# A two-layer hybrid trunk on one core: two low parts of pointwise weights on VectorE, and four pieces of work queued later

## The chip, the core and the metric

The kernel is one program on one core of a Trainium2 chip. The metric is the device time of one execution in microseconds (us). A core has five engines, each of which works through a queue of its own in order: TensorE (PE in the profile; PEld are its weight loads) for matmuls, VectorE (DVE), ScalarE (ACT), GpSimd (POOL), and SyncE (SP), which here only issues transfers. An instruction starts when it is at the head of its queue and the semaphores that it waits for have come.

## The reference

512 positions of 1024 channels pass through two layers. Layer 0 mixes the positions with a gated delta rule (8 heads of 128), layer 1 with a Conformer convolution; each layer then attends to a fixed memory of 256 rows and applies an MLP with a squared ReLU. Every part begins with an RMS norm and ends with a residual sum. All is float32. What the change touches lies around the convolution:

```python
h = h + gated_deltanet(rms_norm(h, dn_norm), ...)                # ends with  o @ w_out
h = h + memory_cross_attention(rms_norm(h, xa_norm[0]), rms_norm(mem, xa_mem_norm[0]), ...)
h = h + sq_relu_mlp(rms_norm(h, mlp_norm[0]), ...)               # square(relu(h @ w_up)) @ w_down
...
u = rms_norm(h, cv_norm) @ w_pw1 + b_pw1                         # 1024 -> 2048
u = u[..., :1024] * sigmoid(u[..., 1024:])
c = causal_depthwise_conv(u, w_dw) + b_dw                        # 31 taps for each channel
c = silu(layer_norm(c, ln_g, ln_b))
h = h + c @ w_pw2 + b_pw2
h = h + memory_cross_attention(rms_norm(h, xa_norm[1]), rms_norm(mem, xa_mem_norm[1]), ...)
```

## The kernel before

**Weights in two parts.** A float32 product is made of three matmuls on a rounded form (fp32r): each operand is split into a high part and a low part, and high x high, low x high and high x low are summed (lines 316 to 318 for activations x weights). The weights come in units of 128 x 1024 (half a block of 1024 x 256). For each unit SyncE loads `raw` (six buffers), ScalarE makes the high part `wh` (a copy with a cast, line 257), and then VectorE or GpSimd makes the low part `wl` = `raw` - `wh` (line 73 is the helper of all elementwise operations on two tensors). There are three buffers of `wh` and `wl` (`NW`), so a cast waits until TensorE has finished with the unit three back. `wnext` hands the next unit of the plan `order` to TensorE and first splits the units up to `ready` ahead; `wsplit` makes one split. `POOL_LO` lists the units whose low part GpSimd makes, counted from `conv0`, the first unit of the convolution's first pointwise product.

**Who sets the order.** Each engine's queue is made by a scheduler that follows the order in which the program issues instructions, within limits: an instruction issued under `tc.issue_after(x)` is not queued ahead of x. `behind_merge` and the entries `ws["rb"]`, `ws["silu"]` and `ws["tap"]` are such gates for casts and low parts. The lists `CONV_SEQ` and `CONV_AFTER` set by hand what is issued after which unit of the convolution's stage.

**The end of the MLP in layer 0.** `mlp7` makes the down projection in four groups of seven products each (`product`); TensorE's matmuls there are `dn`. Their sums `acc` are merged, then `outs` turns them back into the channel layout (`hT`, line 306), adds the residual (`h`), and hands each tile of 128 channels to the norm of the next part: `parts` makes the high part `xh` (ScalarE, line 434) and the low part `xl` (VectorE, line 79), `square` makes the squares and adds them up. `outs(range(4))` runs inside the last product, `outs(range(4, 8))` (called `rest`) inside the first unit of the convolution's pointwise product, between its fourth and fifth k tile. `stat` then makes the norm's factor: matmuls `ssq` (line 453), a root `sd` on ScalarE (line 455), a reciprocal `rb` on VectorE. `mem_gain(1, 0)` and `mem_gain(1, 1)` scale the memory's two halves for the attention of layer 1 (high part `mh` on ScalarE, low part `ml` on VectorE).

**The convolution.** `pw_mm` makes the 16 units of the first pointwise product (`pw`); `pw_ev` evicts one tile of 128 channels: `sg` and `pa` are the two halves times `rb`, `sg` goes through the sigmoid (line 1482). Four tiles are convolved by taps: each tap is one operation on VectorE (`ca`, line 1537) or, for one tile, a ScalarE product and a GpSimd sum (`cvp`, `ca`). The other four go through TensorE: `pw_ev` clears a margin of two columns per phase in `gl` (memset, line 1495), writes the gated tile behind it, ScalarE's queue issues the transfer to DRAM (`gd`, line 1501), SyncE the one back, and `conv` makes the sums by matmuls (`cyp` on VectorE adds the bias). `gl` comes from a pool of three buffers; in this stage `cyp` holds two, so consecutive `gl` use one buffer. While the taps run, TensorE makes K and V of layer 1's attention (`kv_unit`, 16 more units). `moments` makes the layer norm's sums per position; two sums over partitions are matmuls `ln` that TensorE makes inside `kv_unit` at places 27 and 29 of `CONV_SEQ`. Then `ln_out` normalises, and the second pointwise product (`pw2`) begins.

Of the kernel before, what the change touches and what calls it, by code (L numbers as in the profile page):

```python
# [8 lines left out]
F32 = mybir.dt.float32  # L9
F32R = mybir.dt.float32r  # L10
AF = mybir.ActivationFunctionType
# [5 lines left out]
NTAP = 4  # L17
# [21 lines left out]
def tile_trunk(ctx, tc, xT, memT, x_d, mem_d, prm_d, adt_d, bdw_d, tap_d, fin_d, first_d, w_ab, w_kq, w_v, w_z, w_dno, w_pw1, w_pw2,  # L39
# [206 lines left out]
    def wsplit():  # L246
        u = ws["split"]
        ws["split"] += 1
        while ws["load"] <= need[u]:
            wload()  # L250
        (kind, i, *j), hf = order[u]
        raw = combos7(i, j[0], hf) if kind == "dn7" else ws["raw"].pop(need[u])
        h = wp.tile([P, 1024], F32R, tag="wh", name=nm("wh"), bufs=NW)
        lo = wp.tile([P, 1024], F32R, tag="wl", name=nm("wl"), bufs=NW)
        silu = kind == "pw2" and "silu" in ws
        with tc.issue_after(ws["silu" if silu else "rb"].ins) if silu or u in (3, 4) else behind_merge():
            ins = [act.copy(h, raw)]  # L257
        if u < 3:
            tc.keep_in_program_order(ins[0])
        gp = u - conv0 in POOL_LO  # L260
        with tc.issue_after(ws["tap"].ins) if "tap" in ws else nullcontext():
            ins.append(tt(pool if gp else dve, lo, raw, h.bitcast(F32), ALU.subtract))
        if not gp:
            ws["ins"] = ins[1]
        if u < 3:
            tc.keep_in_program_order(ins[1])
        ws["hl"][u] = (h, lo)
        if kind == "dn7":
            after7(i, j[0], hf)

    def wnext(key, hf):
        i = ws["next"]
        assert order[i] == (key, hf), (order[i], key, hf)
        while ws["load"] <= need[min(i + NRAW + 1 + 2 * (order[i][0][0] in ("up", "dn7")), len(order) - 1)]:
            wload()
        ready = NW - (order[i] == (("do", 1), 1)) if i > 2 else (1, 2, 1)[i]
        while ws["split"] < min(i + ready, len(order)):
            wsplit()
        ws["next"] += 1
        return ws["hl"].pop(i)  # L280
# [3 lines left out]
    def behind_merge():  # L284
        return tc.issue_after(ahead[0].ins) if ahead else nullcontext()

    T7 = {}

    def combos7(layer, g, u):
        name, h = order7(layer, g)[u // 2][1], u % 2  # L290
# [68 lines left out]
    def proj_moving(w, hf, q, xs, pss, cs_=None, inside=None):  # L359
        for c, ps in enumerate(pss):  # L360
            if cs_ is not None and c not in cs_:
                continue
            cs = slice(c * P, (c + 1) * P)
            for kk in range(2):
                k = q * 4 + hf * 2 + kk
                xh, xl = xs[k]
                s = slice(kk * 512, (kk + 1) * 512)
                pe.matmul(ps, xh[:, cs], w[0][:, s], start=k == 0, stop=False)
                pe.matmul(ps, xh[:, cs], w[1][:, s], start=False, stop=False)
                pe.matmul(ps, xl[:, cs], w[0][:, s], start=False, stop=k == KT - 1)  # L370
                if inside and c == kk == 0:
                    inside()

    def split(src, s):
        h = slot(F32R, s + "h")
# [48 lines left out]
    class Norm:  # L424
# [6 lines left out]

        def parts(self, t, h, pin=lambda i: i):
            xh = slot(F32R, "xh")
            pin(act.activation(xh, h, AF.Copy, scale=pc(self.g, t)))
            xl = slot(F32R, "xl")
            pin(stt(xl, h, pc(self.g, t), xh.bitcast(F32), ALU.mult, ALU.subtract))
            self.xs.append((xh, xl))

        def square(self, h, e=pool):
            sq = slot(s="sq")  # L440
# [38 lines left out]
    class DeltaNet:  # L479
# [474 lines left out]
        def heads_out(self, hs):  # L954
            pss = [[psum("ogT") for _ in range(2)] for _ in range(2)]
            for k, h in enumerate(hs):
                for c in range(4):
                    turn_in(pss[k // 2], (4 * (k % 2) + c) * 64, self.OG[h // 4, c][:, (h % 4) * P:(h % 4 + 1) * P])
            for k, h in enumerate(hs):
                oh, ol = slot(F32R, "oh"), slot(F32R, "ol")  # L960
                for o, lo, x in zip(by_half(oh), by_half(ol), turned_of(pss[k // 2], k % 2)):
                    act.activation(o, x, AF.Copy, scale=pc("out_norm"))
                    stt(lo, x, pc("out_norm"), o.bitcast(F32), ALU.mult, ALU.subtract)
                os_.append((oh, ol))

        def head_out(self, h):
# [237 lines left out]
    def mlp7(layer, norm, hres, nxt=None, mid=None):  # L1204
# [45 lines left out]
        def dn7(g, ops):  # L1250
# [10 lines left out]
            def product(i):  # L1261
                if (layer, g, i) == (0, 3, 6):
                    outs(range(4))
                left, right, key, opens = order7(layer, g)[i]
                if opens:
                    bank[key] = [psum("dn") for _ in range(2)]
                ws_ = [wnext(("dn7", layer, g), 2 * i)]
                if layer == 1 and (g, i) == (3, 6):
                    ws_.append(wnext(("dn7", layer, g), 13))
                    for h in range(2):  # L1270
                        part(left, ws_[h], bank[key][0], 0, h, opens)
                    held = []
                    evict(right, 0, bank[key][0], held)
                    return last_tile(left, ws_, held[0])
                todo = [(0, 0), (1, 0), (0, 1), (1, 1)]
                for c, h in todo:
                    if h == len(ws_):
                        ws_.append(wnext(("dn7", layer, g), 2 * i + 1))
                    part(left, ws_[h], bank[key][c], c, h, opens)
                    if h == 1:  # L1280
                        evict(right, c, bank[key][c])
# [51 lines left out]
        def outs(tiles):  # L1333
            todo = [(n, c, i) for n in range(2) for c in range(2) for i in tiles]
            pss = [[psum("hT") for _ in range(2)] for _ in range(2)]
            for n, c, i in todo:
                turn_in(pss[i // 2 % 2], (4 * (i % 2) + 2 * n + c) * 64, acc[n, 1 - i // 4, c][:, i % 4 * P:i % 4 * P + P])
            for k, i in enumerate(tiles):
                hn = slot(s="h")
                for o, x, r in zip(by_half(hn), turned_of(pss[i // 2 % 2], i % 2), by_half(hres[i])):  # L1340
                    tt(dve, o, x, r, ALU.add)
                new[i] = hn
                if k:
                    nxt.parts(i - 1, new[i - 1])
            nxt.parts(i, hn)
            for k in range(3) if i == 3 else range(3, 8):
                nxt.square(new[k], pool if i == 3 else dve)

# [107 lines left out]
    def conformer(norm, hres, nxt, rest):  # L1456
# [22 lines left out]
        def pw_ev(m):  # L1479
            sg = slot(s="sg")  # L1480
            tt(dve, sg, st.pop((m, 1)), norm.rb, ALU.mult)
            act.activation(sg, sg, AF.Sigmoid, bias=pc("b_pw1", 8 + m))
            a = slot(s="pa")
            tt(dve, a, st.pop((m, 0)), norm.rb, ALU.mult)
            if m < NTAP:
                x = wp.tile([P, 544], F32, tag="cv", name=nm("xn"), bufs=NCV)[:, 0:542]
                pool.memset(x[:, 0:30], 0.0)
                stt(a, a, pc("b_pw1", m), sg, ALU.add, ALU.mult)
                act.copy(phased(x[:, 30:542]), by_phase(a))
                (todo if m else todo_p).extend((dve_conv if m else pool_conv)(m, x))  # L1490
                return
            gl, x = [t.rearrange("p (j t) -> p j t", t=34) for t in (
                fsp.tile([P, 1024], F32, tag="fs", name=nm("gl"))[:, 0:544],
                wp.tile([P, 544], F32, tag="cv", name=nm("xg"), bufs=NCV))]
            dve.memset(gl[:, :, 0:2], 0.0)
            stt(gl[:, :, 2:34], by_phase(a), pc("b_pw1", m), by_phase(sg), ALU.add, ALU.mult)
            x16[m] = x, gl, drp.tile([P, PH, 34], F32, tag="gd", name=nm("gd"))

# [164 lines left out]
        def ln_out(m):  # L1663
            if m < NTAP:
# [3 lines left out]
                a = slot(s="la")  # L1668
                silu = act.activation(a, ps, AF.Silu, scale=pc("ln_g", m), bias=pc("ln_b", m))
                if m == NTAP - 1:  # L1670
                    ws["silu"] = silu
                return halves_of(a, m % 2 == 0)
            las.extend(slot(s="la") for _ in range(4))
            pss = [[psum("lnT") for _ in range(2)] for _ in range(2)]
# [14 lines left out]
        for i, (kind, u) in enumerate(CONV_SEQ):  # L1689
            if kind == "p":  # L1690
                pw_mm(*divmod(u, 2))
                if u % 2 and u > 1:
                    pw_ev(MORD[u // 2])
            else:
                kv_unit(1, u, lnw.pop("sum", None) if i in LN_SUM else None)

            for ins in gate:
                stack.enter_context(tc.issue_after(ins.ins))
# [216 lines left out]
    for m in range(8):  # L1915
# [1 line left out]
    n2 = Norm("mlp_norm0")  # L1917
    h = xattn(0, n1, h, n2)
    n3 = Norm("cv_norm")
    h, rest = mlp7(0, n2, h, n3, lambda: (mem_gain(1, 0), mem_gain(1, 1), taps(NTAP, *range(9)), selections()))  # L1920
    n4 = Norm("xa_norm1")
    h = conformer(n3, h, n4, rest)
    n5 = Norm("mlp_norm1")
# [49 lines left out]
TAPS_U = (4,) * 7 + (6,) * 9 + (3,) * 8 + (0,) * 8  # L1973
TAPS_C = {4: 0, 5: 0, 6: 0, 7: 0}
SHARE = 5
POOL_LO = (1, 2, 7, 8, 10, 11, 12, 13, 14, 15, 16, 18, 20)
MORD = (0, 1, 4, 2, 5, 3, 6, 7)
CONV_SEQ = [("p", i) for i in range(16)] + [("k", i) for i in range(16)]
CONV_AFTER = [(6, ("w", 4)), (7, ("r", 4)), (10, ("w", 5)), (12, ("r", 5)), (14, ("w", 6)), (15, ("r", 6)), (17, ("w", 7)), (18, ("r", 7)),
# [3 lines left out]
LN_SUM = (27, 29)  # L1983
CONV_AFTER += [(_i, ("t", _m, *range(_a, _a + 3))) for _i, _m, _a in (
    (2, 4, 9), (3, 5, 0), (4, 5, 3), (9, 5, 6), (10, 5, 9), (10, 6, 0), (11, 6, 3), (13, 6, 6), (14, 6, 9), (14, 7, 0), (15, 7, 3),
    (16, 7, 6), (17, 7, 9))]
# [103 lines left out]
```

## Time and profile before

| | |
|---|---|
| median of three runs | 1444.1 us |
| the three runs | 1446.07, 1441.85, 1444.1 us |
| the profiled execution | 1445.35 us |
| its span in the profile | 1443.6 us |
| mean granted clock of TensorE | 0.998 |
| busy share of the span: PE, DVE, ACT, POOL | 99%, 73%, 53%, 17% |

The span runs from the first to the last instruction of the profile; the 1.75 us between it and the profiled execution's time lie around it. Times within the profile are counted from the span's start: the output projection of layer 0's mixer begins at about 327, the first pointwise product at 789, the taps on VectorE at 823, the end of the convolution's stage lies at about 933. A row of a timeline gives the start, the duration, the engine, the line and operation, what is written and read, shapes, and a count where rows are grouped; brackets give the idle time of the engine just before, and what released it. The name `xl` of a helper's line can stand for tiles of several norms, so time and shape tell which is meant.

### The profile page before, as it was taken

What the parts mean: (1) busy time and instruction counts of PE and PEld (TensorE: products, weight loads), DVE (VectorE), ACT (ScalarE), POOL (GpSimd) and SP (SyncE); (2) the same over time, 40 slices, a digit from 0 to 9 for tenths busy, and PEclk for the clock granted to TensorE, in tenths of its full rate; (3) what the DMA queues carried; (4) which work ended last, traced back from release to release, by engine and by line L of the source; (5) the groups of instructions that cost most, each with busy time, mean ns of one, the idle gap of its engine ahead of it and who ended that gap; (6) DMA issues with size and microseconds to landing.
All of it is one profiled execution on the core that took longest, in us unless ns stands there. A gap on an engine that the chain in (4) does not pass through costs nothing.

```text
span 1443.6 us, 20463 instructions
## 1 busy us (share of the span) xinstructions
PE 1429.9 (99%) x7786; PEld 1194.4 (83%) x7786; DVE 1058.0 (73%) x1627; ACT 760.6 (53%) x1279; POOL 246.9 (17%) x246
## 2 busy tenths in 40 slices
PE   9999999999999999999999999999999999999998
PEld 7887888888888888888887887888888888888886
DVE  5989999878555766767679798985555766767677
ACT  6657856655444454444355655574444544444354
POOL 1212200102113010010002377211113010010101
PEclk9999999999999999999999999999999999999999
DMA  8232234522214576575766457743215476585853
GB/s 296 76 117 72 69 96 161 190 86 90 73 47 128 147 180 170 146 204 138 195 165 211 141 162 240 228 146 102 72 46 142 121 179 171 139 211 139 220 151 88
DMA packets 71860, 207.83 MB, mean 144 GB/s; under 512 B 15441, under 2 KB 16593, under 8 KB 71761
## 3 DMA queue, kind: packets, MB, share of 16 engines
q1 hardware_dynamic: 60960, 169.22, 36.0%
q0 software_dynamic: 9792, 35.66, 14.4%
q10 hardware_dynamic: 1008, 1.64, 0.3%
q8 instruction: 61, 1.00, 0.3%
q14 instruction: 39, 0.31, 0.1%
HBM read 203.28 MB, written 3.21 MB: 143 GB/s over the span
## 4 chain that ended last, share of the span: by engine, by line
PE 91%; DVE 6%; ACT 1%; issue 1%; DMA 0%; DVEq 0%; ACTq 0%
PE up L316 8%; PE up L318 8%; PE up L317 8%; PE dn L1259 7%; PE dn L1257 7%; PE dn L1258 7%; DVE ca L1537 3%; PE h L316 3%; PE h L317 3%; PE h L318 3%; PE xo L317 2%; PE q L317 2%; PE q L316 2%; PE xo L316 2%; PE xo L318 2%; PE q L318 2%
## 5 line engine op out<-in xcount | busy, mean ns | idle before, releaser
L257 ACT CAST wh<-raw 128x1024 fp32r<-128x1024 f32 x259 | 271.5, 1051 | 324.4 <-issue 93.8
L73 DVE TENSOR_TENSOR wl<-raw,wh 128x1024 fp32r<-128x1024 f32 (+1 forms) x249 | 307.0, 1235 | 90.0 <-ACT wh L257 88.6
L316 PE MATMUL up<-xh,wh 128*128 128x512 f32 x512 | 199.3, 389 | 0.0
L318 PE MATMUL up<-xh,wl 128*128 128x512 f32 x512 | 199.2, 389 | 0.0
L317 PE MATMUL up<-xl,wh 128*128 128x512 f32 x512 | 199.2, 389 | 0.0
L316 PEld LDWEIGHTS up<-xh,wh 128*128 128x128 f32 x512 | 96.1, 188 | 20.1
L317 PEld LDWEIGHTS up<-xl,wh 128*128 128x128 f32 x512 | 96.1, 188 | 20.0
L318 PEld LDWEIGHTS up<-xh,wl 128*128 128x128 f32 x512 | 96.1, 188 | 19.9
L244 POOL DMA_DIRECT2D t<-w_dn x48 | 42.1, 916 | 376.2 <-DVE wl L73 257.2
L1257 PE MATMUL dn<-wh,ah 128*128 128x512 f32 (+1 forms) x260 | 100.6, 387 | 0.0
L1259 PE MATMUL dn<-wl,ah 128*128 128x512 f32 (+1 forms) x260 | 100.4, 386 | 0.0
L1258 PE MATMUL dn<-wh,al 128*128 128x512 f32 (+1 forms) x260 | 100.4, 386 | 0.0
L79 DVE SCALAR_TENSOR_TENSOR rl<-up,rb 128x512 f32<-128x512 f32 x64 | 44.1, 690 | 58.6 <-PE up L318 58.6
L257 ACT CAST wh<-t 128x1024 fp32r<-128x1024 f32 x44 | 46.4, 1056 | 56.7 <-PE dn L1258 42.0
L73 DVE TENSOR_TENSOR wl<-t,wh 128x1024 fp32r<-128x1024 f32 x44 | 53.7, 1224 | 30.3 <-ACT wh L257 30.1
L1537 DVE SCALAR_TENSOR_TENSOR ca<-xn,prm,ca 128x512 f32<-128x512 f32 x85 | 64.0, 753 | 8.0 <-issue 3.4
L73 POOL TENSOR_TENSOR sq<-sq,sq 128x512 f32<-128x512 f32 x26 | 41.5, 1597 | 156.9 <-ACT sq L441 142.2
L73 DVE TENSOR_TENSOR acc<-acc,dn 128x512 f32<-128x512 f32 x99 | 66.6, 682 | 0.9
L316 PE MATMUL h<-xh,wh 128*128 128x512 f32 x160 | 63.8, 398 | 0.0
L318 PE MATMUL h<-xh,wl 128*128 128x512 f32 x160 | 62.4, 390 | 0.0
L317 PE MATMUL h<-xl,wh 128*128 128x512 f32 x160 | 62.3, 390 | 0.0
L73 DVE TENSOR_TENSOR al<-u,ah 128x512 fp32r<-128x512 f32 x64 | 44.1, 689 | 21.3 <-ACT ah L377 21.3
(427 smaller groups left out, 3508.8 us busy)
## 6 DMA issues: line engine op xcount, KB each, us to landing
raw<-w_dn SPq DMA_DIRECT2D x68, 512.0 KB, 4.6
raw<-w_up SPq DMA_DIRECT2D x64, 512.0 KB, 4.9
t<-w_dn POOLq DMA_DIRECT2D x48, 512.0 KB, 6.6
tap<-tap SPq DMA_DIRECT2D x48, 256.0 KB, 5.6
raw<-w_pw SPq DMA_DIRECT2D x24, 512.0 KB, 4.4
raw<-w_dn POOLq DMA_DIRECT2D x20, 512.0 KB, 7.2
raw<-w_k SPq DMA_DIRECT2D x16, 512.0 KB, 3.8
raw<-w_vv SPq DMA_DIRECT2D x16, 512.0 KB, 5.1
```

Of the source, the lines that this page charges most:

```text
L73: r = e.tensor_tensor(out=o, in0=a, in1=b, op=op)
L79: return dve.scalar_tensor_tensor(out=o, in0=a, scalar=s, in1=b, op0=op0, op1=op1)
L244: nc.gpsimd.dma_start(out=t, in_=a, accum_op=ALU.add)
L257: ins = [act.copy(h, raw)]
L316: pe.matmul(ps, wh, xh, start=first, stop=False)
L317: pe.matmul(ps, wh, xl, start=False, stop=False)
L318: pe.matmul(ps, wl, xh, start=False, stop=last)
L1257: pe.matmul(ps, xh, w[0][:, s], start=opens and k == 0, stop=False, skip_group_check=True)
L1258: pe.matmul(ps, xl, w[0][:, s], start=False, stop=False, skip_group_check=True)
L1259: pe.matmul(ps, xh, w[1][:, s], start=False, stop=k == 3, skip_group_check=True)
L1537: first["tap"] = dve.scalar_tensor_tensor(out=a, in0=src, scalar=w, in1=a, op0=ALU.mult, op1=ALU.add)
```

## The change

Five pieces of work get another place or another engine.

- **Low parts of the first pointwise weights.** `POOL_LO` loses units 1 and 2, so VectorE makes their `wl`. `parts` returns its two instructions, and `outs` puts those of its last tile into a table `behind`: the cast and the low part of unit 1 are issued after `xh` and `xl` of the fourth tile, those of unit 2 after `xh` and `xl` of the eighth. At units `conv0` - 1 and `conv0`, `ready` is one less.
- **The output projection.** The cast and low part of unit ("do", 3), 0 are issued after the last `oh` and `ol` of the heads.
- **The margin memset** of `gl` is issued after `pa` of the same tile.
- **The layer norm's second sum** is issued after the second k tile of its `kv_unit` instead of the first, three matmuls later.
- **Half the memory scaling**, `mem_gain(1, 1)`, is issued in the third product of layer 0's last group instead of in the middle of the MLP.

The gate `ws["silu"]` becomes an entry of `behind`.

```diff
@@ wsplit
-        silu = kind == "pw2" and "silu" in ws
-        with tc.issue_after(ws["silu" if silu else "rb"].ins) if silu or u in (3, 4) else behind_merge():
+        first = behind.get((kind, 0, 0) if kind == "pw2" else (kind, i, hf))
+        if first is None and u in (3, 4):
+            first = [ws["rb"]]
+        with tc.issue_after(first[0].ins) if first else behind_merge():
             ins = [act.copy(h, raw)]
...
-        with tc.issue_after(ws["tap"].ins) if "tap" in ws else nullcontext():
+        low = first[1] if first and len(first) > 1 else ws.get("tap")
+        with tc.issue_after(low.ins) if low else nullcontext():
             ins.append(tt(pool if gp else dve, lo, raw, h.bitcast(F32), ALU.subtract))
@@ wnext
-        ready = NW - (order[i] == (("do", 1), 1)) if i > 2 else (1, 2, 1)[i]
+        ready = NW - (order[i] == (("do", 1), 1) or i in (conv0 - 1, conv0)) if i > 2 else (1, 2, 1)[i]
@@ proj_moving
-                if inside and c == kk == 0:
-                    inside()
+                if inside and (c, kk) == (0, inside[0]):
+                    inside[1]()
@@ the heads' output
-                    act.activation(o, x, AF.Copy, scale=pc("out_norm"))
-                    stt(lo, x, pc("out_norm"), o.bitcast(F32), ALU.mult, ALU.subtract)
+                    behind["do", 3, 0] = [act.activation(o, x, AF.Copy, scale=pc("out_norm")),
+                                        stt(lo, x, pc("out_norm"), o.bitcast(F32), ALU.mult, ALU.subtract)]
@@ product
+                if (layer, g, i) == (0, 3, 2):
+                    mem_gain(1, 1)
@@ outs
-            nxt.parts(i, hn)
+            ins = nxt.parts(i, hn)
+            behind[("pw1", 0, 1) if i == 3 else ("pw1", 1, 0)] = ins
@@ pw_ev
-            tt(dve, a, st.pop((m, 0)), norm.rb, ALU.mult)
+            pa = tt(dve, a, st.pop((m, 0)), norm.rb, ALU.mult)
...
-            dve.memset(gl[:, :, 0:2], 0.0)
+            with tc.issue_after(pa.ins):
+                dve.memset(gl[:, :, 0:2], 0.0)
@@ the call of mlp7
-    h, rest = mlp7(0, n2, h, n3, lambda: (mem_gain(1, 0), mem_gain(1, 1), taps(NTAP, *range(9)), selections()))
+    h, rest = mlp7(0, n2, h, n3, lambda: (mem_gain(1, 0), taps(NTAP, *range(9)), selections()))
@@ tables
-POOL_LO = (1, 2, 7, 8, 10, 11, 12, 13, 14, 15, 16, 18, 20)
+POOL_LO = (7, 8, 10, 11, 12, 13, 14, 15, 16, 18, 20)
-LN_SUM = (27, 29)
+LN_SUM = {27: 0, 29: 1}
```

The scheduler then puts the instructions into the queues as follows. Line numbers are those of each kernel; from line 255 on the new kernel's are a few higher.

VectorE's queue around the third and fourth tile of the norm (`dn` and `acc` are the end of the MLP, `xl` the norm's low parts, `h` the sums with the residual of the next tiles), before:

```order
L73 TENSOR_TENSOR acc_5523<-acc_5523,dn_7541 128x512
L79 SCALAR_TENSOR_TENSOR xl_7527<-h_7515,prm,xh_7525 128x512
L73 TENSOR_TENSOR acc_5531<-acc_5531,dn_7542 128x512
L79 SCALAR_TENSOR_TENSOR xl_7531<-h_7522,prm,xh_7529 128x512
L73 TENSOR_TENSOR h_7643<-hT_7607,h_4741 128x4x64
L73 TENSOR_TENSOR h_7643<-hT_7608,h_4741 128x4x64
```

The same place after (`raw` to `wl` is the low part of unit 1):

```order
L79 SCALAR_TENSOR_TENSOR xl_7527<-h_7515,prm,xh_7525 128x512
L73 TENSOR_TENSOR acc_5523<-acc_5523,dn_7541 128x512
L79 SCALAR_TENSOR_TENSOR xl_7531<-h_7522,prm,xh_7529 128x512
L73 TENSOR_TENSOR acc_5531<-acc_5531,dn_7542 128x512
L73 TENSOR_TENSOR wl_7587<-raw_7411,wh_7586 128x1024
L73 TENSOR_TENSOR h_7639<-hT_7603,h_4741 128x4x64
L73 TENSOR_TENSOR h_7639<-hT_7604,h_4741 128x4x64
```

The low part of unit 1 is new on VectorE, and stands ahead of the sums of the fifth tile; each of the two `xl` has moved ahead of one merge.

ScalarE's queue at the norm's root (`sqh` is the high part of the squares' sum, `sd` the root, `sg` the first sigmoid, `xn` the first tile for the taps, `wh` the casts of pointwise units), before:

```order
L377 CAST sqh_7686<-sq_7533 128x512
L455 ACTIVATE sd_7753<-ssq_7750,eps_rms 128x512
L257 CAST wh_7791<-raw_7561 128x1024
L1482 ACT_TABLE_LOAD
L1482 ACTIVATE sg_7757<-sg_7757,prm 128x512
L257 CAST wh_7848<-raw_7731 128x1024
L1489 COPY xn_7762<-pa_7760 128x16x32
```

After:

```order
L380 CAST sqh_7682<-sq_7533 128x512
L259 CAST wh_7791<-raw_7561 128x1024
L461 ACTIVATE sd_7753<-ssq_7750,eps_rms 128x512
L259 CAST wh_7848<-raw_7731 128x1024
L1491 ACT_TABLE_LOAD
L1491 ACTIVATE sg_7757<-sg_7757,prm 128x512
L1498 COPY xn_7762<-pa_7760 128x16x32
```

Each of the two casts has moved ahead of one activation (the second also ahead of the table load).

VectorE's queue at the last margin memset (`ca` are taps, `cyp` the biases of the convolved tiles, `wl` the low part of a unit of K, `sg` and `pa` the halves of the last gated tile), before:

```order
L79 SCALAR_TENSOR_TENSOR gl_8405<-pa_8403,prm,sg_8400 128x16x32
L1537 SCALAR_TENSOR_TENSOR ca_8493<-xn_8293,prm,ca_8493 128x512 x3
L1495 MEMSET gl_8580 128x16x2
L1537 SCALAR_TENSOR_TENSOR ca_8493<-xn_8293,prm,ca_8493 128x512 x3
L73 TENSOR_TENSOR cyp_7586<-cv_8422,bdw_7588 128x8x32
L73 TENSOR_TENSOR cyp_7587<-cv_8422,bdw_7588 128x8x32
L73 TENSOR_TENSOR wl_8547<-raw_8369,wh_8546 128x1024
```

After:

```order
L79 SCALAR_TENSOR_TENSOR gl_8405<-pa_8403,prm,sg_8400 128x16x32
L1547 SCALAR_TENSOR_TENSOR ca_8493<-xn_8293,prm,ca_8493 128x512 x6
L73 TENSOR_TENSOR wl_8547<-raw_8369,wh_8546 128x1024
L73 TENSOR_TENSOR cyp_7582<-cv_8422,bdw_7584 128x8x32
L73 TENSOR_TENSOR cyp_7583<-cv_8422,bdw_7584 128x8x32
L1547 SCALAR_TENSOR_TENSOR ca_8493<-xn_8293,prm,ca_8493 128x512 x5
L73 TENSOR_TENSOR sg_8575<-pw_8550,rb_7755 128x512
L73 TENSOR_TENSOR pa_8578<-pw_8462,rb_7755 128x512
L1505 MEMSET gl_8580 128x16x2
```

The memset has moved behind `cyp`, five taps, `sg` and `pa`; the low part of K's unit now follows six taps directly. In the same queue the low part of an earlier unit, which stood between the fifth and the sixth tap of a run of nine, stands between the fourth and the fifth.

More of the change, by code (lines that the diff above doesn't have):

```diff
@@ L285, in behind_merge @@
         return tc.issue_after(ahead[0].ins) if ahead else nullcontext()
-    T7 = {}
+    T7, behind = {}, {}
     def combos7(layer, g, u):
@@ L433, in parts @@
             xh = slot(F32R, "xh")
-            pin(act.activation(xh, h, AF.Copy, scale=pc(self.g, t)))
+            ins = [act.activation(xh, h, AF.Copy, scale=pc(self.g, t))]
+            pin(ins[0])
             xl = slot(F32R, "xl")
-            pin(stt(xl, h, pc(self.g, t), xh.bitcast(F32), ALU.mult, ALU.subtract))
+            ins.append(stt(xl, h, pc(self.g, t), xh.bitcast(F32), ALU.mult, ALU.subtract))
+            pin(ins[1])
             self.xs.append((xh, xl))
+            return ins
         def square(self, h, e=pool):
@@ L1670, in ln_out @@
                 if m == NTAP - 1:
-                    ws["silu"] = silu
+                    behind["pw2", 0, 0] = [silu]
                 return halves_of(a, m % 2 == 0)
@@ L1694, in conformer @@
             else:
-                kv_unit(1, u, lnw.pop("sum", None) if i in LN_SUM else None)
+                kv_unit(1, u, (LN_SUM[i], lnw.pop("sum")) if i in LN_SUM else None)
             for ins in gate:
```

## Prediction

> **What bounds the kernel now.** I read the page first, then the waits of TensorE, then the timelines of the four engines around the two longest of those waits.
>
> ```profile
> span 1443.6 us, 20463 instructions
> PE 1429.9 (99%) x7786; PEld 1194.4 (83%) x7786; DVE 1058.0 (73%) x1627; ACT 760.6 (53%) x1279; POOL 246.9 (17%) x246
> ```
>
> TensorE (PE) is busy for 1429.9 of 1443.6 us, so no reordering can bring more than 13.7 us, plus what matmuls lose at a lower clock. The change does not touch the matmuls themselves. So I ask only which of TensorE's waits go, and what is late next.
>
> ```profile
> PE K L318 <- DVE wl L73: 2.7, 1, 2.7
> PE pw L317 <- DVE xl L79: 1.8, 1, 1.8
> PE do L316 <- ACT oh L962: 0.2, 1, 0.2
> PE ln L1644 <- DVE lw L73: 0.2, 1, 0.2
> PE dn L1259 <- DVE wl L73: 0.2, 1, 0.2
> ```
>
> Each row is a wait of TensorE (engine, tile, line, releaser; total, times, longest). All five lie where the diff moves something; the other waits of the list, in the first 15 us and at 0.2, it leaves alone. Together they are 5.1 us, and behind the longest the clock falls:
>
> ```profile
> 892.00:896.00 4.00, 1.88 (x11) 1.89 (x12) 3.93 (x4) 0.00 (x0) 3.21 (x2) 0.84 1.03 354
> 896.00:898.00 2.00, 2.00 (x11) 2.00 (x11) 1.93 (x4) 0.00 (x0) 0.00 (x0) 0.50 0.97 291
> ```
>
> These are two stretches by windows; the third number from the end of the line is the granted clock. It is 0.84 over 4 us and 0.50 over the next 2, so 0.16 x 4 + 0.50 x 2 = 1.6 us are lost after the wait as well. At the same time VectorE (DVE) is busy 3.93 of 4 us: in this stage it, not TensorE, is the engine that is full.
>
> **The first pointwise weights (two subtractions from GpSimd to VectorE).**
>
> ```profile
> 790.31 0.39 PE L318 MATMUL pw<-xh,wl 128*128 128x512 f32 x1
> 790.54 0.39 PE L316 MATMUL pw<-xh,wh 128*128 128x512 f32 x1
> 791.05 0.50 PE L317 MATMUL pw<-xl,wh 128*128 128x512 f32 x1
> 791.63 0.40 PE L316 MATMUL pw<-xh,wh 128*128 128x512 f32 x1
> 793.83 0.50 PE L317 MATMUL pw<-xl,wh 128*128 128x512 f32 x1 [1.80 <-DVE xl L79]
> ...
> 789.35 1.64 DVE L79 SCALAR_TENSOR_TENSOR xl<-h,prm,xh 128x512 fp32r<-128x512 f32 x1
> 791.52 2.25 DVE L79 SCALAR_TENSOR_TENSOR xl<-h,prm,xh 128x512 fp32r<-128x512 f32 x1
> 797.16 0.75 DVE L79 SCALAR_TENSOR_TENSOR xl<-h,prm,xh 128x512 fp32r<-128x512 f32 x1
> ...
> 787.75 2.69 POOL L73 TENSOR_TENSOR wl<-raw,wh 128x1024 fp32r<-128x1024 f32 x1 [11.62 <-ACT wh L257]
> 790.62 2.60 POOL L73 TENSOR_TENSOR wl<-raw,wh 128x1024 fp32r<-128x1024 f32 x1 [0.18 <-ACT wh L257]
> 793.19 3.08 POOL L73 TENSOR_TENSOR sq<-sq,sq 128x512 f32<-128x512 f32 x2
> ```
>
> The same VectorE operation takes 0.75 us alone, but 1.64 and 2.25 beside GpSimd (POOL): it ends 0.55 us after GpSimd's subtraction ends (787.75 + 2.69 = 790.44, and 789.35 + 1.64 = 790.99; then 793.22 and 793.77). TensorE's two starts that wait for it come 0.51 and 2.20 us after the matmul before them, where 0.23 is usual (790.54 - 790.31); so 0.28 + 1.97 = 2.25, about 2.3 us, are lost. With GpSimd idle there, both tiles are ready in time, and these 2.3 us go.
>
> The Trainium skill (SBUF — State Buffer, Who interferes with whom) says that VectorE with two SBUF inputs and a GpSimd instruction that reads SBUF exclude each other for a whole instruction. The trace agrees: the ends above lie 0.55 us behind GpSimd's. By it the moved subtractions, which have two SBUF inputs too, shut GpSimd out in turn, which speaks against the change; the rows price that below, at up to 1.2 us.
>
> Added to VectorE are two subtractions of about 1.24 us (the row at 841.17 below). The first follows the fourth tile, in time for TensorE, but it holds back GpSimd's two square sums (3.08 us), which then run into VectorE's next xl tile; I put 0.5 us of wait on that (0 to 1.2). The second comes ahead of the squares that feed the norm's sum, on a chain that TensorE's `ssq` matmuls wait for; `ssq` also stands later in TensorE's order, so I put 0.1 there (0 to 2.5, both subtractions in full).
>
> **Gates for the output projection's cast and half the memory scaling.** These remove the `do` and `dn` waits, 0.2 us each; at 793.83 a listed wait of 1.80 cost 1.97, so I count about 0.35 each, 0.7 together (0.4 to 0.8). The scaling's second half meets ScalarE and VectorE work one product later, where no wait of TensorE is listed: nothing, or at worst the 0.2 of `dn` comes back.
>
> TensorE's lead when the convolution begins is then 0.7 + 2.3 - 0.6 = 2.4 us (1.0 to 3.1).
>
> **What the moved casts cost.** On ScalarE (ACT) the sixth and seventh pointwise casts now stand ahead of the root and of the first sigmoid's table load, instead of behind each.
>
> ```profile
> 810.10 1.05 ACT L257 CAST wh<-raw 128x1024 fp32r<-128x1024 f32 x1 [1.85 <-PE pw L317]
> 811.17 1.28 ACT L1482 ACT_TABLE_LOAD   x1
> 813.35 0.73 ACT L1482 ACTIVATE sg<-sg,prm 128x512 f32<-128x512 f32 x1 [0.89 <-DVE sg L73]
> 815.54 1.05 ACT L257 CAST wh<-raw 128x1024 fp32r<-128x1024 f32 x1 [1.47 <-PE pw L317]
> 816.50 1.11 ACT L1489 COPY xn<-pa 128x512 f32<-128x512 f32 x1
> ```
>
> The cast at 815.54 waits until TensorE has finished with a buffer. In the new order the table load (1.28), the sigmoid (0.73), VectorE's product (0.75 as the xl above) and then `xn` queue behind it: `xn` starts at 815.54 + 1.05 + 1.28 + 0.73 + 0.75 + 0.1 for the handovers = 819.45, less TensorE's lead of 2.4, so 817.05 instead of 816.50. VectorE's taps, released by that chain, start 0.55 us later than before (2.95 less the lead: between -0.15 and 1.95).
>
> **The margin memset.**
>
> ```profile
> 882.64 2.34 DVE L1537 SCALAR_TENSOR_TENSOR ca<-xn,prm,ca 128x512 f32<-128x512 f32 x3
> 888.42 0.72 DVE L1537 SCALAR_TENSOR_TENSOR ca<-xn,prm,ca 128x512 f32<-128x512 f32 x1 [3.44 <-issue]
> 888.42 0.09 DVE L1495 MEMSET gl<- 128x32 f32 x1
> 891.29 2.77 DVE L73 TENSOR_TENSOR wl<-raw,wh 128x1024 fp32r<-128x1024 f32 x1
> ...
> 882.70 0.33 ACTq L1501 DMA_DIRECT2D gd<-gl  x1
> ...
> 882.08 8.59 POOL L73 TENSOR_TENSOR ca<-ca,cvp 128x512 f32<-128x512 f32 x6
> 890.62 2.36 POOL L73 TENSOR_TENSOR wl<-raw,wh 128x1024 fp32r<-128x1024 f32 x1
> ...
> 891.10 0.28 PE L317 MATMUL K<-ml,wh 128*128 128x256 f32 x1
> 894.12 0.39 PE L318 MATMUL K<-mh,wl 128*128 128x256 f32 x1 [2.73 <-DVE wl L73]
> ```
>
> VectorE stands still for 3.44 us, and the first to go on is a 0.09 us memset of `gl`. The trace names no releaser ("issue"), but the buffer is the one that the transfer issued at 882.70 still reads. Behind the memset wait three taps, `cyp` and the subtraction `wl` whose end (894.06) is TensorE's start (894.12). Queued after `pa`, some 10 us later, the memset finds the transfer done: VectorE gains 3.4 us. The subtraction now comes directly after six taps; it meets one of GpSimd's additions (8.59 / 6 = 1.43 each), so it waits 0.5 (0 to 1.4) and takes 1.24, where it now takes 2.77: 1.0 more gained (0.1 to 1.5).
>
> **One place where VectorE loses.**
>
> ```profile
> 823.08 11.84 DVE L1537 SCALAR_TENSOR_TENSOR ca<-xn,prm,ca 128x512 f32<-128x512 f32 x15 [1.99 <-ACT ca L1534]
> 837.35 3.91 DVE L1537 SCALAR_TENSOR_TENSOR ca<-xn,prm,ca 128x512 f32<-128x512 f32 x5
> 841.17 1.24 DVE L73 TENSOR_TENSOR wl<-raw,wh 128x1024 fp32r<-128x1024 f32 x1
> 837.03 4.30 POOL L73 TENSOR_TENSOR ca<-ca,cvp 128x512 f32<-128x512 f32 x3 [4.56 <-ACT cvp L1520]
> 843.18 0.39 PE L318 MATMUL pw<-xh,wl 128*128 128x512 f32 x1
> ```
>
> This subtraction moves ahead of the fifth tap, from 841.17 to 840.4. There GpSimd's third addition runs until 841.33, so it waits: 0.8 us (0 to 0.9). TensorE wants its result at 843.18 less 2.4 and gets it at 842.4 + 0.55 or so: a new wait of about 2.2 us that eats most of TensorE's lead. It costs nothing by itself if VectorE sets the end of the stage.
>
> The layer norm's second sum moves three matmuls later; it has no listed wait of its own (the 0.2 at `ln` is one wait, of the first sum), so I count nothing.
>
> **The sum.** From the taps on VectorE is nearly always busy, and TensorE waits for its moments at `ln`. Past the split at 894.06 TensorE would be ahead by its 2.9 us (894.12 less 891.22, half a spacing of 0.23 after the 256-wide matmul at 891.10) and the 1.6 us of clock, 4.5; VectorE by 3.4 + 1.0 - 0.8 - 0.55 = 3.05, less 0.15 for ScalarE, whose copy of GpSimd's sum waits for additions that are not earlier (0 to 0.8). The smaller lead is what reaches `ln` and the end: 2.9 us. The profiled execution took 1445.35 us (1443.6 of it the span), the median is 1444.1; 2.9 less gives 1442.45 for such an execution and 1441.2 for the median, which I forecast. With all terms at their worst 3.4 + 0.1 - 0.9 - 1.95 - 0.8 = -0.15, at their best 3.4 + 1.5 + 0.15 = 5.05 us of gain, held by TensorE's 4.5 unless its own lead is left.
>
> **Rivals.**
> - TensorE gets all: 0.7 + 2.3 - 0.6 + 2.9 + 1.6 = 6.9 us, 1437.2. It needs VectorE not to be the limit at `ln`; for it speaks that TensorE waits there only 0.2, against it that this wait exists at all. The middle way, in which VectorE's two moved subtractions meet no GpSimd instruction, gives up to 5.05 us, 1439.05. Together 0.25. The Trainium skill (TensorE: Matmul & The Clock Gate, Part 1: The HAM clock gate) lets the clock fall after an idle window of about 3.4 us; by it the 2.73 us wait would not have cost the 1.6, and the first of these two would be 5.3 us, 1438.8. Here the clock fell behind 2.73, so the measurement decides.
> - The start is eaten: TensorE loses its lead at the square sums, and the taps begin 2 us later or more. The gain is 2.9 - 2.4 = 0.5 us plus whatever lead is left. At a lead of 0 to 1 it is 0.5 to 1.5: 1443.1. Chance 0.14.
> - Slower: the same mechanism past its turning point. If TensorE waits at `ssq` for more than 2.9 us beyond the forecast, its lead is below -0.5 and the total turns into a loss. A wait of 3 us there, about the length that halved the clock, would cost 1.6 us more: 2.4 - 3 - 1.6 = -2.2, so 1.7 us slower, 1445.8. For it: two subtractions of 1.24 and the later order on one chain. Against: `ssq` stands later, too. Chance 0.07.
> - That the memset doesn't stall any more but the transfer does: the next write of `gl` needs the same buffer, but some 10 us later, and the transfer issued at 882.70 was over at 888.42, when the first memset ran. Part of the forecast's low end.
>
> **How the numbers follow.** Forecast 0.54, the larger gains 0.25, the eaten start 0.14, slower 0.07. A measurement of this kernel can tell about 0.3%, 4.3 us, from no change. The forecast itself is within that; I give a fifth of it and of the middle way's lower part to sampling (the three runs lie 4.2 us apart). So faster by over 0.3%: 0.29; within: 0.64; slower: 0.07. The range runs from just below the middle way to the eaten start: 1438.5 to 1443.8.
>
> **What would show it.** Right: no 3.44 us gap before the memset; no row `K <- DVE wl` and a granted clock of 1.00 after it; xl tiles of 0.75 us; a new wait of about 2 us for a `wl` near 841; taps that start at 823 to 824. Wrong: a wait of TensorE at `ssq` over 1 us, a K wait that comes back, or a lead at `ln` that differs from VectorE's.

## The result and the profile after

The changed kernel takes 1440.2 us (median of 8 runs, 1439.24 to 1440.39) against 1443.97 us of the kernel before (8 runs, 1441.85 to 1446.07): 0.9971 of its time, 95% interval 0.9961 to 0.9982, so 3.8 us faster (2.6 to 5.6). Timed once more on another chip it is 0.9972 (0.9963 to 0.9982). 1441.2 us was forecast, in a range of 1438.5 to 1443.8; the gain of 0.29% lies at the bound of what was to be told from no change.

The head of the page after:

```profile
span 1437.5 us, 20460 instructions
PE 1426.3 (99%) x7786; PEld 1191.4 (83%) x7786; DVE 1053.9 (73%) x1629; ACT 760.8 (53%) x1279; POOL 242.6 (17%) x244
```

The two profiled spans lie 6.1 us apart, more than the medians: the profiled execution before (1445.35 us) lies 1.4 us above its median, the one after (1439.24 us) 1.0 below its own. 1.2 of the 6.1 us come in the first 12 us, where in this execution ScalarE's first cast, which waits for a transfer, starts at 4.39 instead of 4.85 and the early matmuls take 0.39 us instead of 0.63; the change does not touch that part, and the later profiles are 0.3 to 1.2 us ahead of the kernel before there, too. Rows of TensorE's waits after:

```profile
PE pw L321 <- DVE wl L73: 2.1, 1, 2.1
...
PE h L1793 <- ACT xh L437: 0.5, 1, 0.5
PE pw L321 <- POOL wl L73: 0.5, 1, 0.5
```

The five waits that the prediction listed (K, pw for xl, do, ln, dn) are all gone. In their place stand two new ones in the convolution's stage, for low parts: one of VectorE (2.1 us), one of GpSimd (0.5 us). (The wait at `h` lies in the first 15 us.) How TensorE's lead grows and shrinks is read by taking the start of the same matmul in both timelines:

| matmul | before | after | lead, less the 1.2 of the start | step |
|---|---|---|---|---|
| `do` that waited | 326.83 | 325.19 | 0.4 | +0.4 |
| `dn` that waited | 761.35 | 759.38 | 0.8 | +0.3 |
| `pw` with xl of the fourth tile | 793.83 | 789.40 | 3.2 | +2.5 |
| `pw` with wl of unit 9 (VectorE) | 843.18 | 840.93 | 1.0 | -2.2 |
| `pw` with wl of unit 13 (GpSimd) | 868.86 | 867.43 | 0.2 | -0.8 |
| `K` that waited | 894.12 | 889.97 | 2.9 | +2.7 |
| `K`, past the half clock of before | 898.08 | 892.37 | 4.5 | +1.6 |
| `V`, behind the second `ln` | 939.64 | 933.46 | 5.0 | +0.5 |

So TensorE earned 3.2 us up to the convolution's first unit and gave 3.0 of them back while the taps ran. Of the gain that is left, near 5 us in this pair, 4.3 are what the memset's stall had cost: 2.7 of wait and 1.6 of clock. The rows behind these steps, in the order of time. The norm's third and fourth xl on VectorE, the low part of unit 1 behind them, and GpSimd's first work there:

```profile
786.71 0.74 DVE L79 SCALAR_TENSOR_TENSOR xl<-h,prm,xh 128x512 fp32r<-128x512 f32 x1
787.97 0.75 DVE L79 SCALAR_TENSOR_TENSOR xl<-h,prm,xh 128x512 fp32r<-128x512 f32 x1
789.23 1.22 DVE L73 TENSOR_TENSOR wl<-raw,wh 128x1024 fp32r<-128x1024 f32 x1
...
789.63 3.35 POOL L73 TENSOR_TENSOR sq<-sq,sq 128x512 f32<-128x512 f32 x2 [15.45 <-ACT sq L447]
```

With GpSimd idle the xl tiles take 0.74 and 0.75 us where they took 1.64 and 2.25. ScalarE's two moved casts:

```profile
805.40 1.05 ACT L259 CAST wh<-raw 128x1024 fp32r<-128x1024 f32 x1 [1.54 <-PE pw L320]
806.35 0.68 ACT L461 ACTIVATE sd<-ssq,eps_rms 128x512 f32<-128x512 f32 x1
811.07 1.05 ACT L259 CAST wh<-raw 128x1024 fp32r<-128x1024 f32 x1 [4.04 <-issue]
812.14 1.28 ACT L1491 ACT_TABLE_LOAD   x1
813.44 0.72 ACT L1491 ACTIVATE sg<-sg,prm 128x512 f32<-128x512 f32 x1
814.98 1.12 ACT L1498 COPY xn<-pa 128x512 f32<-128x512 f32 x1 [0.82 <-DVE pa L79]
```

The second cast stands at the head of the queue for 4.04 us; the trace names no releaser, but the cast needs a buffer that TensorE still reads. Table load, sigmoid and `xn` wait behind it. Unit 9, on VectorE, GpSimd and TensorE:

```profile
838.87 2.00 DVE L73 TENSOR_TENSOR wl<-raw,wh 128x1024 fp32r<-128x1024 f32 x1
...
835.51 4.29 POOL L73 TENSOR_TENSOR ca<-ca,cvp 128x512 f32<-128x512 f32 x3 [4.56 <-ACT cvp L1530]
...
840.93 0.50 PE L321 MATMUL pw<-xh,wl 128*128 128x512 f32 x1 [2.06 <-DVE wl L73]
```

The subtraction takes 2.00 us, since GpSimd's third addition runs until 839.80. And the place of the memset:

```profile
821.56 3.13 DVE L1547 SCALAR_TENSOR_TENSOR ca<-xn,prm,ca 128x512 f32<-128x512 f32 x4 [1.98 <-ACT ca L1544]
...
881.43 4.71 DVE L1547 SCALAR_TENSOR_TENSOR ca<-xn,prm,ca 128x512 f32<-128x512 f32 x6 [0.59 <-ACT ca L1544]
886.05 1.22 DVE L73 TENSOR_TENSOR wl<-raw,wh 128x1024 fp32r<-128x1024 f32 x1
887.19 0.75 DVE L73 TENSOR_TENSOR cyp<-cv,bdw 128x256 f32<-128x256 f32 x2
887.85 2.33 DVE L1547 SCALAR_TENSOR_TENSOR ca<-xn,prm,ca 128x512 f32<-128x512 f32 x3
```

Six taps run through, and the low part for K is ready at 887.3, 2.7 us ahead of TensorE's start at 889.97; the clock stays at 1.00:

```profile
886.00:892.00 6.00, 6.00 (x48) 5.84 (x47) 5.86 (x10) 1.68 (x2) 5.84 (x4) 1.00 0.78 206
892.00:898.00 6.00, 6.00 (x99) 5.54 (x101) 4.79 (x8) 5.26 (x7) 2.60 (x3) 1.00 1.01 346
```

### The profile page after: what moved, and what is told of

It reads as the page before. It is cut to its first block, busy times and chain, and to the rows that moved or that the text cites. A ratio compares the mean times of both kernels' runs of the same rounds, so it can differ in the third digit from the quotient of the medians.

```text
span 1437.5 us, 20460 instructions
## 1 busy us (share of the span) xinstructions
PE 1426.3 (99%) x7786; PEld 1191.4 (83%) x7786; DVE 1053.9 (73%) x1629; ACT 760.8 (53%) x1279; POOL 242.6 (17%) x244
## 3 DMA queue, kind: packets, MB, share of 16 engines
q10 hardware_dynamic: 1008, 1.64, 0.3%
## 4 chain that ended last, share of the span: by engine, by line
PE 94%; DVE 3%; ACT 1%; issue 1%; POOL 1%; DMA 0%; SPq 0%; DVEq 0%; POOLq 0%; ACTq 0%
PE up L319 8%; PE up L320 8%; PE up L321 8%; PE dn L1263 7%; PE dn L1264 7%; PE dn L1265 7%; PE h L319 3%; PE h L320 3%; PE h L321 3%; PE xo L320 2%; PE q L320 2%; PE q L321 2%; PE xo L319 2%; PE xo L321 2%; PE q L319 2%; PE pw L319 2%
```

## The experiments

Theory A: what TensorE gains ahead of the taps is given back at low parts for which it then waits, because the casts that the split moves start VectorE's and GpSimd's queues late; the memset's gate alone carries the gain. Theory B: savings on TensorE add up and are kept, the split's among them. The first four kernels were timed beside each other (kernel before: 1445.17 us), and so were the last four (1444.98 us).

**All but the memset's gate.**

```diff
-            with tc.issue_after(pa.ins):
-                dve.memset(gl[:, :, 0:2], 0.0)
+            dve.memset(gl[:, :, 0:2], 0.0)
```

> The changed kernel with the margin memset where it stood before; all other parts stay. Theory A (what TensorE gains ahead of the taps is given back at low parts that it then waits for, so the memset's gate alone carries the gain): VectorE is no more than 0.8 us ahead of the kernel before when it meets the memset, the stall of about 3.4 us, TensorE's wait at K of 2 to 2.7 us and the half clock behind it all come back, and of the gain only 0.4 to 1.2 us are left: 1442.8 to 1443.6 us. Theory B (savings on TensorE add up; those ahead of the taps are 3.2 us and are kept): 3.2 to 3.6 us faster than before, 1440.3 to 1440.8 us.

1444.61 us, 0.9993 of the kernel before (0.9984 to 1.0002): 1.0 us faster by the ratio, which is not told from no change and is what theory A says; 3.2 us would be outside the interval. The stall is back, and here the trace names what was only inferred from the kernel before, the transfer out of the same buffer:

```profile
887.44 0.09 DVE L1504 MEMSET gl<- 128x32 f32 x1 [3.99 <-DMA gd<-gl]
```

TensorE's waits in this kernel, one where the split's gain ends and one at K, a little shorter than the 2 to 2.7 us that were expected there (the clock had also fallen behind the first, so that TensorE came 1.6 us later):

```profile
PE pw L321 <- DVE wl L73: 2.0, 1, 2.0
PE K L321 <- DVE wl L73: 1.7, 1, 1.7
```

**The gate alone.** The kernel before, with that gate put in.

> The kernel before with the memset's gate and nothing else. Theory A: nearly the whole gain of the change: no stall of VectorE, no wait at K, no fall of the clock, 2.8 + 1.5 = 4.3 us less a new wait of 0 to 0.5 at the low part of unit 9; the 2.3 us at the first pointwise unit and the waits at do, dn and the second layer norm sum stay. 3.8 to 4.4 us faster than before in the trace, 1439.6 to 1440.2 us if the time follows. Theory B: 4.8 less the 3.2 and 0.4 of the other parts, 1.2 us faster: about 1442.8 us.

1441.41 us, 0.9974 (0.9963 to 0.9984): 3.8 us, against 4.2 (0.9971) of the whole change at that base. Its trace, less 0.4 us at the start, is 4.1 us ahead of the kernel before past the half clock. The waits that the other parts remove are still there:

```profile
PE pw L317 <- DVE xl L79: 1.8, 1, 1.8
...
PE do L316 <- ACT oh L962: 0.2, 1, 0.2
...
PE ln L1645 <- DVE lw L73: 0.2, 1, 0.2
PE dn L1259 <- DVE wl L73: 0.2, 1, 0.2
```

One line of five changed pieces makes nearly all of the gain. It also moves the low part of unit 9 one tap ahead: that shift, which the prediction charged to the change as a whole, is the gate's.

**Unit 9 one tap later.** In the changed kernel the low part of unit 9 is issued after the tap behind which it stood before.

```diff
+        if u - conv0 == 9:
+            ws["late"] = lambda: ws.update(ins=tt(dve, lo, raw, h.bitcast(F32), ALU.subtract))
+            ws["hl"][u] = (h, lo)
+            return
...
                 first["tap"] = dve.scalar_tensor_tensor(out=a, in0=src, scalar=w, in1=a, op0=ALU.mult, op1=ALU.add)
+                if "late" in ws:
+                    ws["n9"] = ws.get("n9", 0) + 1
+                    if ws["n9"] == 6:
+                        with tc.issue_after(first["tap"].ins):
+                            ws.pop("late")()
```

> The changed kernel with the low part of unit 9 on VectorE one tap later, where it stood before. Theory A: TensorE waits there as long as now (2.06 us by the trace, within 0.2), since the subtraction begins when GpSimd's third addition ends, in either order; VectorE gains the 0.8 us, which TensorE does not get: within 0.5 us of the changed kernel. Theory B: the wait comes from the place in the queue; it falls by 0.8 us or more, and the kernel is 0.8 to 2 us faster than the changed one.

The wait is as long as in the changed kernel. The subtraction no longer stands still for GpSimd's addition (1.23 us instead of 2.00), but the tap ahead of it fills the same time, and it ends at 841.18 instead of 840.87 in an execution that starts 0.3 us later:

```profile
839.95 1.23 DVE L73 TENSOR_TENSOR wl<-raw,wh 128x1024 fp32r<-128x1024 f32 x1
...
835.79 4.30 POOL L73 TENSOR_TENSOR ca<-ca,cvp 128x512 f32<-128x512 f32 x3 [4.54 <-ACT cvp L1534]
...
841.23 0.50 PE L325 MATMUL pw<-xh,wl 128*128 128x512 f32 x1 [2.07 <-DVE wl L73]
```

So the place in the queue is not the cause of the wait, as theory A says, though not by its reason: the subtraction comes when VectorE gets there, not when GpSimd ends. With all but the gate, where unit 9 stands at its old place too, the wait is the same 2.0 us. What the place does cost is GpSimd's time: its low part for unit 13 begins at 864.54 instead of 864.99, 0.7 us earlier with the starts set off, and TensorE's wait at unit 13 is gone. The time is less plain: 1438.96 us, 0.9956 (0.9943 to 0.9968), 1.4 us below the changed kernel's 1440.34 on the other base, where at most 0.5 was expected; the intervals overlap. The trace shows 0.7 of it, behind unit 13; the rest is open. It may be the clock, which fell behind this wait in one profile of the changed kernel and not here (below).

**The casts back.** In the changed kernel the casts of units 5 and 6 are issued after the root and after the first sigmoid, where they stood before.

```diff
+        if u - conv0 in (5, 6):
+            first = [ws["sd" if u - conv0 == 5 else "sig"]]
...
```

> The changed kernel with the casts of units 5 and 6 behind the root and behind the first sigmoid again, as before; all else stays. Theory A: the first tile for the taps and with it VectorE's and GpSimd's queues come 1.4 us earlier (1.0 to 1.8), the wait of 2.06 us at unit 9 falls to about 0.8, and as what TensorE gives back at the low parts of units 9 and 13 is set by those two engines, the kernel ends about 1.4 us earlier than the changed one (1.0 to 1.8). Theory B: the order on ScalarE is off the path; within 0.4 us of the changed kernel.

1438.26 us, 0.9949 (0.9936 to 0.9961): 7.4 us faster than the kernel before. It is faster than the changed kernel too, by 2.1 us in the medians: its interval ends at 0.9961, where those of the changed kernel begin (0.9961 and 0.9963), and its slowest run (1438.62) lies below all 17 of the changed kernel (1439.24 and more). ScalarE's queue:

```profile
805.71 0.69 ACT L463 ACTIVATE sd<-ssq,eps_rms 128x512 f32<-128x512 f32 x1 [1.75 <-PE ssq L461]
806.30 1.04 ACT L261 CAST wh<-raw 128x1024 fp32r<-128x1024 f32 x1
807.36 1.28 ACT L1493 ACT_TABLE_LOAD   x1
811.50 0.72 ACT L1493 ACTIVATE sg<-sg,prm 128x512 f32<-128x512 f32 x1 [2.86 <-DVE sg L73]
812.12 1.04 ACT L261 CAST wh<-raw 128x1024 fp32r<-128x1024 f32 x1
813.07 1.10 ACT L1500 COPY xn<-pa 128x512 f32<-128x512 f32 x1
```

The table load now lies in the time in which ScalarE waits for VectorE, and `xn` starts at 813.07 instead of 814.98. Every tap is 1.9 us earlier, to the last one; so is the matmul of unit 9, whose wait is gone from the list, and the end of the span (1435.7 against 1437.5 us). The size was expected at 1.4 (1.0 to 1.8); the mechanism is theory A's. The two casts were not tried one by one.

**The changed kernel again.**

> The changed kernel as it is, timed beside the other three, since the median of the kernel before moves by about 1 us from chip to chip. Theory A and theory B both: 0.997 of the kernel before, as the first time, or slightly less (0.9960 to 0.9975).

1440.34 us, 0.9972 (0.9963 to 0.9982).

**All but the split.**

```diff
-POOL_LO = (7, 8, 10, 11, 12, 13, 14, 15, 16, 18, 20)
+POOL_LO = (1, 2, 7, 8, 10, 11, 12, 13, 14, 15, 16, 18, 20)
...
-        ready = NW - (order[i] == (("do", 1), 1) or i in (conv0 - 1, conv0)) if i > 2 else (1, 2, 1)[i]
+        ready = NW - (order[i] == (("do", 1), 1)) if i > 2 else (1, 2, 1)[i]
...
-            ins = nxt.parts(i, hn)
-            behind[("pw1", 0, 1) if i == 3 else ("pw1", 1, 0)] = ins
+            nxt.parts(i, hn)
```

> The changed kernel with the low parts of units 1 and 2 on GpSimd again and all that goes with it undone (the two gates and the one less in ready), so that the memset, the output projection, the second layer norm sum and the memory scaling are changed alone. Theory A (the split gains 2.3 us at the first pointwise unit, and the casts that it moves on ScalarE give them back through the start of the taps): as fast as the changed kernel, within 0.6 us, with the waits for xl back (1.8 us listed) and the wait at unit 9 gone. Theory B (the split's gain is kept): 2 to 2.5 us slower than the changed kernel.

1440.87 us, 0.9975 (0.9966 to 0.9983), the changed kernel's time. The casts stand where they stood, the wait at unit 9 is not in the list, and the lock of the two engines is back, with VectorE's xl beside GpSimd's low parts:

```profile
787.48 1.65 DVE L79 SCALAR_TENSOR_TENSOR xl<-h,prm,xh 128x512 fp32r<-128x512 f32 x1
...
789.65 2.25 DVE L79 SCALAR_TENSOR_TENSOR xl<-h,prm,xh 128x512 fp32r<-128x512 f32 x1
...
785.88 2.70 POOL L73 TENSOR_TENSOR wl<-raw,wh 128x1024 fp32r<-128x1024 f32 x1 [11.55 <-ACT wh L259]
788.74 2.62 POOL L73 TENSOR_TENSOR wl<-raw,wh 128x1024 fp32r<-128x1024 f32 x1 [0.16 <-ACT wh L259]
```

The three pieces that are left beside the gate show in this trace, with 0.8 us at `do` and `dn` and 0.3 at the second `ln`, but not in the time: the ratio is close to that of the gate alone (0.9974).

**The split alone.** The kernel before with the new `POOL_LO`, the two gates behind `parts` and the one less in `ready`.

> The kernel before with the split alone: units 1 and 2 on VectorE, their gates, the one less in ready; nothing else. Theory A: the waits for xl go (2.3 us), a wait of about 2 us at unit 9 comes, the memset's stall and TensorE's wait at K stay: within 0.6 us of the kernel before. Theory B: 2 to 2.5 us faster than before.

1445.3 us, 1.0002 (0.9994 to 1.0010): nothing, where theory B wants 2 us or more. The waits show the exchange (the first rows of the list):

```profile
PE K L321 <- DVE wl L73: 3.3, 1, 3.3
PE pw L321 <- DVE wl L73: 2.0, 1, 2.0
PE K L321 <- POOL wl L73: 1.3, 1, 1.3
```

What is saved at xl is lost at unit 9, and what is not lost there makes the wait at K longer. The clock stays up behind that wait, which is worth 1.5 us here, and the third wait, for GpSimd's low part, takes them back. Theory B falls.

**The casts back and unit 9 later.** Both edits together.

> The changed kernel with the casts of units 5 and 6 put back and the low part of unit 9 one tap later. Theory A: what is left of the waits ahead of K is one for GpSimd's low part of unit 13 (0.5 us listed, 0.8 lost); with VectorE 0.8 us earlier the lock between the two engines falls otherwise and half of it goes: 0.3 to 0.5 us faster than with the casts alone, 6.5 to 7.5 us faster than the kernel before. Theory B: GpSimd's own pace sets that wait: no difference to the casts alone.

1437.39 us, 0.9950 (0.9936 to 0.9963), the same as with the casts alone. In the traces the second edit is worth 0.7 us: this execution starts 0.8 us later (at 122 us), and is level at unit 13, where no wait is listed any more. The ratios cannot tell 0.7 us, so between the two theories this run leaves open whether it pays. This kernel and that with the casts back are the fastest of all.

## Why the prediction was right, and where its steps were not

The forecast sum was 2.9 us, the smaller of two leads past the split for K: TensorE's 4.5 and VectorE's 2.9. TensorE's came out at 4.5, as forecast. VectorE's came out at 4.5 too (its last tap starts at 911.73 instead of 917.42, 5.7 less the 1.2 of the start), so that neither holds up the other. By the medians the gain is 3.8 us. That the forecast of 2.9 lies so near to it is in part luck: the sum is 1.6 us short of what this pair of profiles shows, the pair shows more than the medians, and the interval of 2.6 to 5.6 us does not tell the two apart.

- **The step that failed** is VectorE's sum, and in it above all this term: "VectorE's taps, released by that chain, start 0.55 us later than before". They start 0.3 us earlier (821.56 against 823.08, less the 1.2). The chain behind the cast was right to the hundredth: 3.91 us from the cast to `xn` forecast (819.45 - 815.54), 814.98 - 811.07 = 3.91 measured. TensorE's lead, by which the cast comes earlier, was too small: 2.4 forecast, 3.3 measured.
- That lead: `do` and `dn` gave 0.8 (0.7 forecast), the waits for xl 2.5 (2.3 forecast). The 0.6 us that were set against it, for GpSimd's square sums and the second subtraction, came to 0.15 at most: the sums take 3.35 us, and no wait is listed at `ssq`.
- The memset gave VectorE 3.4 us, as forecast; the low part for K behind it 1.5 (1.0 forecast, best case 1.5): GpSimd's additions do not hold it up, and it takes 1.22 us.
- The term for ScalarE's copy of GpSimd's sum came out at 0.45 (0.15 forecast, at worst 0.8): the copy waits 0.35 us for the last addition, and VectorE waits 1.21 us for the cast behind it, where it waited 0.76.
- Unit 9 costs VectorE 0.8 us, and TensorE waits 2.06 there, both as forecast (0.8 and about 2.2). But "it costs nothing by itself" does not quite hold. In the second profile the clock fell behind this wait; 1.5 us were lost by it, and 0.5 of them were still missing at the end.
- Not foreseen: the same shift makes GpSimd 0.8 us later, so TensorE gives back 0.8 us at GpSimd's low part of unit 13 (with unit 9 one tap later that wait is gone). Nor was it foreseen that VectorE gains 0.5 us near 870, where one product takes 0.82 us beside GpSimd instead of 1.30. VectorE's sum is then 0.3 - 0.8 + 0.5 + 3.4 + 1.5 - 0.45 = 4.45.
- The moved `ln` was counted at nothing, on the ground that the listed 0.2 belonged to the first sum. It belonged to the second, at 938.65 us, and 0.4 to 0.5 us came.
- The rival in which the start is eaten did not happen at the square sums. TensorE's lead went later: 2.2 us at unit 9, as the forecast had it, and 0.8 at unit 13.
- The rival in which TensorE gets all (6.9 us) needed VectorE's and GpSimd's queues to start earlier as well. With the casts back they do, and that trace ends 6.7 us ahead of the kernel before, with 1.2 us of the start set off.
- By the Trainium skill (SBUF — State Buffer, Who interferes with whom), VectorE with two SBUF inputs and a GpSimd instruction that reads SBUF exclude each other. The traces agree, with 0.75 against 2.25 us for the same xl.

## What to carry to other kernels

A stage that another engine paces takes back what the bound engine brings into it; so before a wait ahead of such a stage is priced, ask whether the pacing engines' queues start earlier too, and undo the parts one at a time, since the title's edit can be worth nothing and a side edit all. When a gate or a look-ahead is changed, read what it moves on the engine that nobody speaks of: here two casts moved ahead of a root and a table load on ScalarE, and cost 1.9 us. A clear of a reused buffer belongs behind work that needs its engine anyway, not at the head of a queue where it waits for a transfer.

## What was not expected of the hardware

The length of TensorE's wait does not by itself decide whether its clock falls behind it. Windows of 4 us behind the wait at unit 9, in the changed kernel's first profile and in its second, where the list has the same 2.06 us:

```profile
842.00:846.00 4.00, 4.00 (x19) 3.16 (x17) 3.89 (x7) 0.66 (x2) 2.40 (x2) 1.00 0.71 217
```

```profile
842.00:846.00 4.00, 4.00 (x13) 3.09 (x12) 3.86 (x7) 0.07 (x1) 2.94 (x2) 0.57 0.66 198
```

The clock is 1.00 in the one, 0.57 in the other; 0.43 x 4 = 1.7 us were lost. With all but the gate it fell behind 2.05 us of wait at unit 9 and again behind 1.73 us at K (0.57 from 893 to 897), and with the split alone it did not fall behind 3.27 us:

```profile
893.38 0.39 PE L321 MATMUL K<-mh,wl 128*128 128x256 f32 x1 [3.27 <-DVE wl L73]
...
893.00:897.00 4.00, 3.62 (x53) 3.49 (x56) 3.86 (x6) 0.00 (x0) 1.47 (x1) 1.00 0.87 301
```

The Trainium skill (TensorE: Matmul & The Clock Gate, Part 1: The HAM clock gate) asks for an idle window of about 3.4 us; waits of 1.73, 2.05, 2.06 and 2.73 us were enough here, and once 3.27 were not. So the 1.6 us that the prediction counted for the clock are a loss that some executions have and others not. The spread of the runs may go with it, which is not shown: the kernels with a wait of TensorE at the memset's place spread by 4.2 to 5.6 us (8 to 27 runs), those without by 1.2 to 3.2 (5 to 12 runs).

What decides it, the traces show in part. Each half clock in the convolution's stage lasts 3.41 us (894.73 to 898.14 before; 842.20 to 845.61 and 893.40 to 896.81 with all but the gate; 842.10 to 845.51 in the changed kernel's second profile), and the two with all but the gate begin 51.20 us apart, 15 times that length. That fits a clock that is set anew in windows of 3.41 us, which lie elsewhere in every execution. Here are the windows around unit 9, counted in each execution from a change of its clock, in the changed kernel's first profile and in its second:

```profile
837.21:840.62 3.41, 1.66 (x8) 1.04 (x6) 3.34 (x4) 1.89 (x3) 3.33 (x4) 1.00 0.58 108
840.62:844.03 3.41, 3.10 (x13) 2.55 (x14) 3.27 (x6) 0.00 (x0) 3.41 (x2) 1.00 0.53 160
```

```profile
838.69:842.10 3.41, 1.35 (x7) 0.81 (x6) 3.37 (x4) 1.00 (x2) 3.33 (x4) 1.00 0.54 82
842.10:845.51 3.41, 3.41 (x10) 2.63 (x9) 3.27 (x6) 0.00 (x0) 2.84 (x2) 0.50 0.63 197
```

The same wait is cut into 1.75 and 0.31 us in the first and lies whole in one window, with 2.06 idle, in the second. By this count half clock followed windows with 2.74, 2.06, 2.05 and 1.73 us idle, and did not follow those with 1.81 (a part of the 3.27), 1.75 and 1.54. So the bound is somewhere near 1.7 to 1.8 us of a window, an estimate from these seven; the order of the nearest three is not clean, the ends of matmuls are modelled, and no run was made to test it.
